# Scaling the residual rows during the up projection, with the second half's rows in buffers of their own

## The chip, the core and the metric

The kernel runs on one core of a Trainium2 chip. The core has five engines with instruction queues of their own: PE (matrix products; "PEld" in the profile is its loading of weights), DVE (elementwise work on vectors), ACT (activation functions and copies), POOL (elementwise work too) and SP, which computes nothing and issues DMA transfers. ACT and POOL can issue transfers as well. Each queue runs in order: an instruction that waits holds up everything behind it on the same engine. Engines wait for one another through semaphores.

The metric is device time in microseconds (us) of one execution.

## The reference

A trunk of two layers over 1024 tokens of 1024 features, in 32-bit floats. Layer 0 mixes with a gated delta rule, layer 1 with retention; each is followed by a feed-forward block with a short causal convolution. Every residual sum goes through a layer norm with a gain row `ln_g` and a bias row `ln_b`:

```
for i in range(2):
    sh1, sc1, g1, sh2, sc2, g2 = split(e @ ada_w[i] + ada_b[i], 6)
    y = mixers[i](x * (1 + sc1) + sh1)
    x = layer_norm(ALPHA * x + (1 + g1) * y, ln_g[i, 0], ln_b[i, 0])
    y = conv_ffn(x * (1 + sc2) + sh2, ffn_up[i], ffn_conv_w[i], ffn_conv_b[i], ffn_down[i])
    x = layer_norm(ALPHA * x + (1 + g2) * y, ln_g[i, 1], ln_b[i, 1])

def conv_ffn(h, w_up, conv_w, conv_b, w_down):
    gate, up = split(h @ w_up, 2)
    return (silu(causal_dwconv(gate, conv_w) + conv_b) * up) @ w_down
```

The point of the change is the `x` inside `ALPHA * x` of the second layer norm of each layer. What the kernel stores after the first norm is the normalized rows without gain and bias (`x_mid`, tensors `xs`), because the product that follows can take the gain into its own scale. The residual sum after the down projection needs the rows with gain and bias: x = n * g + b, row by row. Somebody has to compute that, for 1024 rows in each layer.

## The kernel before

**Products.** Each 32-bit product is made of three passes: a value is split into a coarse part (ACT, line 89) and the rest (DVE, line 90), and PE multiplies low by high, high by low and high by high. The large products use a seven-product scheme (Strassen and Winograd) on blocks of 512.

**Up projection** (`strassen`, called by `layer_tail`). It goes through 22 items, eleven pairs of a gate item and an up item. The first two are handled apart; the items from 2 on run in `wino`. An item loads two weight blocks into `wr` (lines 1223 and 1224, two buffers), forms seven products of 12 matmuls each, and hands four quarters to a `sink`. A gate item ends in the convolution (DVE line 1568), an up item in the gated quarters `o`, their four sums and differences on POOL (line 1589) and seven stores to DRAM (`ad`, line 1573, issued by SP). Twice in each item `bg_step` does one unit of background work from a list `bg`, for example a strip of the conditioning product `ada` (lines 215 to 243).

**Down projection** (`proj_gen`). Seven products over `nj` = 11 blocks, in the order 11, S1, S2, S4, 12, S3, 22. For each block SP loads a piece of the stored activations (`ar`, line 1274) and, three steps ahead, a piece of the weights (`Bw`, `Br`, line 1307); DVE forms differences (lines 1315 to 1321) and both are split. After each product its four accumulators are evacuated (`f1` to `f7`); the lines that matter are 1414 (`f3`), 1399 (`f2`) and 1421 (`f7`). The queue order of each engine is not written out by hand: a scheduler orders the instructions by program order and its own estimate of when each is ready, so that loads are often issued long before the place where they are written. `issue_after` (here `after(key)`) holds an instruction behind a named one on the same queue.

**The residual rows.** For the first half (512 rows) `xload(0, t)` loads four tiles of 128 rows from `x_mid` in the third product (S2), and DVE applies gain and bias in place, four operations for each tile (line 1357). For the second half `gain_half` (lines 1343 to 1350), eight times in the fourth and fifth products, loads 128 x 512 values into a buffer of the tag `xT` (two buffers), lets POOL multiply and add, and has POOL store them to the scratch tensor `xg`. `xload(1, t)` loads them back from `xg` in the sixth product, into the four buffers of the tag `lane`, which hold the first half's rows until these are stored. The gain rows are four tiles of the tag `auh` (eight buffers). That tag also serves the rows of the gate `rows[i, 5]`, the rotary tables `trig` (line 1636) and others.

`finish(half, t, nh, c)` then forms ALPHA * x + g * y (line 1364) and the norm's statistics, and `norm` normalizes; in the last layer (`final`) it also applies the output's gain and bias and stores the result.

For layer 1's first sum another route exists already: `bg_gain` puts 16 units into the background list; each loads 128 x 512 values into a `lane` buffer, scales them on POOL and has SP store them to `xg`.

Of the kernel before, what the change touches and what calls it, by code (L numbers as in the profile page):

```python
# [33 lines left out]
def trunk_kernel(ctx: ExitStack, tc, A):  # L34
# [84 lines left out]
    def bg_step(tile=mm_tile):  # L119
        bg_ps[0] = tile  # L120
        for p in pend:
            p[0] -= 1
        while pend and (pend[0][0] <= 0 or not bg):
            pend.pop(0)[1]()
            if not bg:
                break
        if bg:
            nxt = bg.pop(0)()
            if nxt:
                pend.append(list(nxt))  # L130

# [249 lines left out]
    def bg_gain(n, src, dst):  # L381
        gb = []

        def unit(c, r):
            if r == 0:
                gb[:] = [tl("auh", [P, HALF], name="gb") for _ in range(2)]
                for t, nm in zip(gb, ("ln_g", "ln_b")):
                    sp.dma_start(t, A[nm][n:n + 1, hs(c)].to_broadcast([P, HALF]))
            x = tl("lane", [P, HALF], name="xg")
            rs = slice(r * P, r * P + P)  # L390
            sp.dma_start(x, src[rs, hs(c)])
            if r == 7:
                return gain(x, rs, c)
            return 1, lambda: gain(x, rs, c)

        def gain(x, rs, c):
            pool.tensor_tensor(x, x, gb[0], ALU.mult)
            pool.tensor_tensor(x, x, gb[1], ALU.add)
            sp.dma_start(dst[rs, hs(c)], x)

        for c in range(2):
            for r in range(8):
                bg.append(lambda c=c, r=r: unit(c, r))
# [757 lines left out]
    def strassen(hT0, xts, scale, shift, items, tags=("hTb", "hTb", "qkv", "qkv", "aux"), direct=False):  # L1161
# [58 lines left out]
        def wino(n, sink):  # L1220
            ua, ub = items[n][:2]
            wa, wb = tl("wr", [P, D]), tl("wr", [P, D])
            sp.dma_start(wa, ua)
            sp.dma_start(wb, ub)
# [24 lines left out]
            bg_step()  # L1249

# [27 lines left out]
    def proj_gen(nj, ablk, wsrc, slots, xsrc, G, final, ln_next, tag, ltags, dst, key, mm=pe.matmul, gate=None, gain=None):  # L1278
# [62 lines left out]
        grows = gain_rows(gain[0], key) if gain else None  # L1341

        def gain_half(n):
            hf, rs = n // 4, slice(HALF + n % 4 * P, HALF + (n % 4 + 1) * P)
            x = tl("xT", [P, HALF], name="xg")
            with after("w"):
                sp.dma_start(x, gain[1][rs, hs(hf)])
            for r, op in zip(grows, (ALU.mult, ALU.add)):
                pool.tensor_tensor(x, x, r[hf], op)
            pool.dma_start(xsrc[rs, hs(hf)], x)  # L1350

        def xload(half, t):
            xt = load_row(xsrc if half or not gain else gain[1], half, t)
            if half == 0 and gain:
                for r, op in zip(grows, (ALU.mult, ALU.add)):
                    for hf in range(2):
                        dve.tensor_tensor(xt[:, hs(hf)], xt[:, hs(hf)], r[hf], op)
            xts[half].append(xt)
            stats[half].append(tl("st", [P, 2, 6]))

        def finish(half, t, nh, c):
            dve.tensor_tensor(c, c, G[nh], ALU.mult)
            xv = xts[half][t][:, hs(nh)]
# [3 lines left out]
        def norm(half, t):  # L1367
# [7 lines left out]
            else:  # L1375
# [3 lines left out]
                lo, hi = xt[:, hs(0)], xt[:, hs(1)]  # L1379
# [71 lines left out]
        for p, (an, bn, fin, side, fresh) in enumerate(prods):  # L1451
# [8 lines left out]
            for j in range(nj):  # L1460
# [8 lines left out]
                if gain and p in (3, 4) and j % 2 == 0 and j < 8:  # L1469
                    gain_half((p - 3) * 4 + j // 2)  # L1470
                if gain and p == 2 and j % 2 == 0 and j < 8:
                    xload(0, j // 2)
                if p == 2 and j < 4 and gate:
# [30 lines left out]
            if p == 4:  # L1504
                hooks = [] if final else ln_hooks(0, xts[0], tag, ln_next, outs, dst, key, bal["h"])
                hooks += [lambda t=t: xload(1, t) for t in range(4)]
# [12 lines left out]
    def layer_tail(i, mix, wout, xsrc, x_mid, x_out, ln_next, final):  # L1519
# [14 lines left out]
        bg_ada(i, 5, "row")  # L1534
        if i == 0:
# [7 lines left out]
        def pair_items(fp):  # L1543
# [31 lines left out]
            def up_start():  # L1575
                seen = []

                def gated(q, a, b):
# [7 lines left out]
                    if len(seen) == 4:  # L1586
# [8 lines left out]
        strassen(hT0, xts, sc2, sh2, [it for fp in range(NF // 2) for it in pair_items(fp)])  # L1595
        slots = {"c": "hTa", "x": "qkv"}
        gb2 = gain_rows(3, ("mid", i), "hTb") if final else None
        return proj_st(proj_gen(NF // 2, ablk_of(ad, "qkv"), A["ffn_down"][i], slots, xg[i + 1], rows[i, 5],
                       (gb2, x_out) if final else None, ln_next, "hTb", ("hTb", "hTa", 8, 6, "f") if final else ("qkv", "hTa", 8, 4, "0"), x_out, ("out", i), gain=(2 * i, x_mid)))
# [358 lines left out]
```

## Time and profile before

| what | value |
|---|---|
| median of 3 runs | 2968.27 us (2963.58 to 2969.49) |
| the profiled execution | 2955.5 us, of which the span of its instructions is 2953.7 us |
| granted TensorE clock, mean | 0.984 |
| PE busy / idle in the span | 2816.4 us / 137.3 us |
| DVE, ACT, POOL busy | 2243.3, 1318.0, 451.1 us |
| up projection, layer 0 and 1 | about 795 to 1193 us and 2325 to 2735 us |
| down projection, layer 0 and 1 | about 1193 to 1430 us and 2735 to 2935 us |

How to read the rows that follow. A row of the stage windows gives a stretch of the span, its length, then the busy time and number of instructions of PE, PEld, DVE, ACT and POOL, the granted clock, the share of the DMA engines' time in use, and GB/s. A row of the timeline gives start, duration, engine, line, operation and tiles (`out<-in`); a bracket at its end is the idle time before it and what ended that. A row of the waits reads "engine line <- what it waited for: total, times, longest". In the chain of waits each row is a start, a duration and the piece of work on the path that ended last. "SPq" is SP's queue. Tiles of one tag share a number of buffers; a new tile waits until an older one is released.

### The profile page before, as it was taken

Reading aid. Unit: us, or ns where it says so; the run is one execution under the profiler, and the core shown is the slowest. Engines: PE = TensorE matmul, PEld = TensorE weight load, DVE = VectorE, ACT = ScalarE, POOL = GpSimd, SP = SyncE. Lnnn points to the kernel's source line nnn. Section 1 sums busy time; section 2 is a strip of 40 time slices with the busy share of each in tenths; the row PEclk is TensorE's granted clock in tenths of the full one; section 3 lists DMA queues with packets and bytes.
Section 4 is the critical chain, followed back from the end, with each engine's and each line's share of the span. In section 5 each row is a group of like instructions: output and inputs, shape, how many; then the busy total and the mean of one; then the engine's idle time right before and its main releaser. Section 6 shows DMA issues by size and latency. Waiting matters only on the chain.

```text
span 2953.7 us, 38896 instructions
## 1 busy us (share of the span) xinstructions
PE 2816.4 (95%) x13638; PEld 2303.2 (78%) x13638; DVE 2243.3 (76%) x4005; ACT 1318.0 (45%) x2413; POOL 451.1 (15%) x469
## 2 busy tenths in 40 slices
PE   8998898999999999999999999999999899999997
PEld 7887777887788888877878877777777788888885
DVE  5788787656688888968676756666689787777989
ACT  4745565444544444545333333222244544445443
POOL 0302221100001111140000022422202011111211
PEclk9999999999999999999999999999999999999999
DMA  7231222254244445765343364755654343324763
GB/s 277 86 111 65 83 79 80 83 168 158 92 160 163 150 162 174 286 225 175 131 147 121 109 229 144 222 169 177 198 204 146 103 136 107 107 102 159 278 205 136
DMA packets 244403, 451.01 MB, mean 153 GB/s; under 512 B 23088, under 2 KB 76592, under 8 KB 244208
## 3 DMA queue, kind: packets, MB, share of 16 engines
q1 hardware_dynamic: 213088, 401.07, 41.1%
q10 hardware_dynamic: 29760, 43.00, 4.0%
q0 software_dynamic: 1360, 4.46, 0.4%
q8 instruction: 107, 1.75, 0.2%
q14 instruction: 88, 0.72, 0.1%
HBM read 339.91 MB, written 108.53 MB: 152 GB/s over the span
## 4 chain that ended last, share of the span: by engine, by line
PE 77%; DVE 9%; DMA 6%; ACT 4%; issue 2%; POOL 1%; SPq 0%; POOLq 0%; ACTq 0%; DVEq 0%
PE acc L655 15%; PE acc L1167 10%; PE acc L110 6%; PE acc L111 6%; PE acc L112 6%; PE sc L1167 5%; PE acc L1441 4%; PE sc L655 4%; PE mm L655 2%; PE sc L111 2%; PE sc L112 2%; PE sc L110 2%; PE mm L658 1%; DMA Br<-in_ffn_down 1%; PE acc L314 1%
## 5 line engine op out<-in xcount | busy, mean ns | idle before, releaser
L655 PE MATMUL acc<-hT,wh 128*128 128x512 f32 x960 | 300.1, 394 | 0.0
L1441 PE MATMUL acc<-bb,ab 128*128 128x512 f32 x984 | 233.4, 395 | 9.7 <-DVE bb L90 7.0
L1589 POOL TENSOR_TENSOR o<-o 128x512 f32<-128x512 f32 x80 | 112.3, 1414 | 793.6 <-DVE o L1582 494.0
L1441 PEld LDWEIGHTS acc<-bb,ab 128*128 128x128 f32 x984 | 183.7, 189 | 54.0 <-DVE bb L90 11.8
L1167 PE MATMUL acc<-T,wb 128*128 128x512 f32 x840 | 202.9, 390 | 6.5 <-DVE wb L90 6.5
L655 PEld LDWEIGHTS acc<-hT,wh 128*128 128x128 f32 x960 | 182.2, 190 | 34.1
L89 ACT ACTIVATE ab<-ar 128x512 fp32r<-128x512 f32 x210 | 130.4, 627 | 174.1 <-PE mm L291 57.4
L655 PE MATMUL acc<-hT,wl 128*128 128x512 f32 x480 | 201.2, 419 | 0.0
L1167 PEld LDWEIGHTS acc<-T,wb 128*128 128x128 f32 x840 | 157.0, 188 | 42.9 <-DVE wb L90 9.8
L90 DVE TENSOR_TENSOR wl<-wr,wh 128x1024 fp32r<-128x1024 f32 x95 | 123.3, 1298 | 81.9 <-ACT wh L89 81.6
L90 DVE TENSOR_TENSOR ab<-ar,ab 128x512 fp32r<-128x512 f32 x210 | 159.7, 765 | 30.0 <-ACT ab L89 29.9
L90 DVE TENSOR_TENSOR wb<-mm,wb 128x512 fp32r<-128x512 f32 x216 | 146.0, 684 | 26.4 <-ACT wb L89 25.5
L89 ACT ACTIVATE wh<-wr 128x1024 fp32r<-128x1024 f32 x95 | 100.8, 1062 | 142.8 <-PE acc L655 66.4
L90 DVE TENSOR_TENSOR wb<-wr,wb 128x512 fp32r<-128x512 f32 x162 | 110.5, 687 | 69.0 <-ACT wb L89 68.8
L1228 ACT ACTIVATE pc<-acc 128x512 f32<-128x512 f32 x143 | 84.9, 594 | 163.1 <-PE acc L1167 108.8
L1568 DVE SCALAR_TENSOR_TENSOR o<-g,vc,o 128x512 f32<-128x512 f32 (+2 forms) x176 | 145.6, 844 | 6.2 <-ACT o L1563 5.5
L89 ACT ACTIVATE wb<-mm 128x512 fp32r<-128x512 f32 x216 | 123.9, 595 | 53.8 <-DVE mm L1217 49.3
L89 ACT ACTIVATE wb<-wr 128x512 fp32r<-128x512 f32 x162 | 99.8, 629 | 99.7 <-DMA wr<-in_ffn_up 36.4
L655 PE MATMUL acc<-wh,hT 128*128 128x512 f32 x384 | 137.4, 420 | 2.9 <-DVE vv L90 1.7
L110 PE MATMUL acc<-T,wb 128*128 128x512 f32 x292 | 115.6, 396 | 9.4 <-DVE wb L90 9.4
L476 DVE SCALAR_TENSOR_TENSOR qkv<-raw,vc,qkv 128x512 f32<-128x512 f32 x144 | 111.7, 780 | 11.4 <-ACT qkv L474 10.7
L111 PE MATMUL acc<-T,wb 128*128 128x512 f32 x292 | 115.1, 394 | 0.0
(641 smaller groups left out, 7428.6 us busy)
## 6 DMA issues: line engine op xcount, KB each, us to landing
wr<-in_ffn_up SPq DMA_DIRECT2D x92, 512.0 KB, 4.2
mvw<-in_ada_w SPq DMA_DIRECT2D x80, 512.0 KB, 4.1
ad<-o SPq DMA_DIRECT2D x154, 256.0 KB, 3.1
ar<-ad SPq DMA_DIRECT2D x154, 256.0 KB, 4.8
Br<-in_ffn_down SPq DMA_DIRECT2D x88, 256.0 KB, 4.3
wr<-in_ret_wv SPq DMA_DIRECT2D x32, 512.0 KB, 4.1
ar<-od SPq DMA_DIRECT2D x56, 256.0 KB, 5.4
xs<-xt ACTq DMA_DIRECT2D x24, 512.0 KB, 3.6
```

What stands on the lines that cost most here:

```text
L89: act.activation(dst_h, src, AF.Copy)
L90: eng.tensor_tensor(dst_l, src, dst_h, ALU.subtract)
L110: mm(acc, wl[:, k], hl[0], start=first, stop=False)
L111: mm(acc, wh[:, k], hl[1], start=False, stop=False)
L112: mm(acc, wh[:, k], hl[0], start=False, stop=last)
L476: dve.scalar_tensor_tensor(oh, raw[:, 3 - j:515 - j], w[:, 3 - j:4 - j], oh, ALU.mult, ALU.add)
L655: pq(pe.matmul(out, lhsT, rhs, start=start, stop=stop), cost)
L1167: return pe.matmul(*a, skip_group_check=True, **kw)
L1228: act.activation(t, X, AF.Copy)
L1441: return pe.matmul(*args, skip_group_check=True, **kw)
L1568: dve.scalar_tensor_tensor(tv, gv[:, c0 - j:c1 - j], w[:, 2 - j:3 - j], tv, ALU.mult, ALU.add)
L1589: (dve if fp == 0 else pool).tensor_tensor(o[d], o[x], o[y], op)
```

## The change

Five things are done:

1. `bg_gain` gets a tag. With the tag `xT` its units go to a list of their own, `rowq`; their loads (and those of the gain rows) are held behind the current item's second weight load (`anchor["wi"]`), and POOL issues their stores.
2. `layer_tail` calls it with `x_mid` and `xg[i + 1]`, so that all 1024 rows of each layer are scaled; `row_step` takes one unit at the end of each item from number 5 on, and anything left after the last item.
3. `proj_gen` loses its `gain` parameter, the gain rows, `gain_half` and the scaling on DVE. Both halves are loaded from `xg`.
4. The first two tiles of the second half go into `xT` buffers.
5. In the last layer the second half is loaded in the fourth product (S4) in place of the sixth, and its other two tiles go into pairs of `auh` buffers.

```
+    rowq, rowp = [], []
+
+    def row_step():
+        if rowp:
+            rowp.pop()()
+        if rowq:
+            nxt = rowq.pop(0)()
+            if nxt:
+                rowp.append(nxt[1])
...
-    def bg_gain(n, src, dst):
+    def bg_gain(n, src, dst, tag="lane"):
...
-                for t, nm in zip(gb, ("ln_g", "ln_b")):
-                    sp.dma_start(t, A[nm][n:n + 1, hs(c)].to_broadcast([P, HALF]))
-            x = tl("lane", [P, HALF], name="xg")
+                with after("wi") if tag == "xT" else nullcontext():
+                    for t, nm in zip(gb, ("ln_g", "ln_b")):
+                        sp.dma_start(t, A[nm][n:n + 1, hs(c)].to_broadcast([P, HALF]))
+            x = tl(tag, [P, HALF], name="xg")
             rs = slice(r * P, r * P + P)
-            sp.dma_start(x, src[rs, hs(c)])
+            with after("wi") if tag == "xT" else nullcontext():
+                sp.dma_start(x, src[rs, hs(c)])
...
-            sp.dma_start(dst[rs, hs(c)], x)
+            (sp if tag == "lane" else pool).dma_start(dst[rs, hs(c)], x)
...
-                bg.append(lambda c=c, r=r: unit(c, r))
+                (bg if tag == "lane" else rowq).append(lambda c=c, r=r: unit(c, r))
...
-            sp.dma_start(wb, ub)
+            anchor["wi"] = sp.dma_start(wb, ub)
...
             bg_step()
+            if n > 4:
+                row_step()
...
-        grows = gain_rows(gain[0], key) if gain else None
-
-        def gain_half(n):
-            hf, rs = n // 4, slice(HALF + n % 4 * P, HALF + (n % 4 + 1) * P)
-            x = tl("xT", [P, HALF], name="xg")
-            with after("w"):
-                sp.dma_start(x, gain[1][rs, hs(hf)])
-            for r, op in zip(grows, (ALU.mult, ALU.add)):
-                pool.tensor_tensor(x, x, r[hf], op)
-            pool.dma_start(xsrc[rs, hs(hf)], x)
...
-            xt = load_row(xsrc if half or not gain else gain[1], half, t)
-            if half == 0 and gain:
-                for r, op in zip(grows, (ALU.mult, ALU.add)):
-                    for hf in range(2):
-                        dve.tensor_tensor(xt[:, hs(hf)], xt[:, hs(hf)], r[hf], op)
-            xts[half].append(xt)
+            if half and t < 2:
+                x = load_row(xsrc, half, t, tag="xT")
+            elif half and final:
+                x = two("auh", F32, "xt")
+                r0 = HALF + t * P
+                for hf in range(2):
+                    with after("w"):
+                        sp.dma_start(x[hf], xsrc[r0:r0 + P, hs(hf)])
+            else:
+                x = load_row(xsrc, half, t)
+            xts[half].append(x)
...
-                if gain and p in (3, 4) and j % 2 == 0 and j < 8:
-                    gain_half((p - 3) * 4 + j // 2)
-                if gain and p == 2 and j % 2 == 0 and j < 8:
+                if not gate and p == 2 and j % 2 == 0 and j < 8:
                     xload(0, j // 2)
+                if final and p == 3 and j % 2 == 0 and j < 8:
+                    xload(1, j // 2)
...
-                hooks += [lambda t=t: xload(1, t) for t in range(4)]
+                if not final:
+                    hooks += [lambda t=t: xload(1, t) for t in range(4)]
...
         bg_ada(i, 5, "row")
+        bg_gain(2 * i, x_mid, xg[i + 1], "xT")
...
         strassen(hT0, xts, sc2, sh2, [it for fp in range(NF // 2) for it in pair_items(fp)])
+        while rowq or rowp:
+            row_step()
...
-                       (gb2, x_out) if final else None, ln_next, ..., x_out, ("out", i), gain=(2 * i, x_mid)))
+                       (gb2, x_out) if final else None, ln_next, ..., x_out, ("out", i)))
```

A small helper `xh(half, t, nh)` picks the half of a row tile, whether it is one tile or a pair.

More of the change, by code (lines that the diff above doesn't have):

```diff
@@ L1276, in ablk_of, with proj_gen @@
         return ablk
-    def proj_gen(nj, ablk, wsrc, slots, xsrc, G, final, ln_next, tag, ltags, dst, key, mm=pe.matmul, gate=None, gain=None):
+    def proj_gen(nj, ablk, wsrc, slots, xsrc, G, final, ln_next, tag, ltags, dst, key, mm=pe.matmul, gate=None):
         bal = {nm: BAL[ltags[4] + nm] for nm in ABLK + ("w11", "w21", "w22", "wT1", "wT2", "wT3", "wT4", "n", "h")}
@@ L1340, in proj_gen, with xh @@
         stats = [[], []]
-        grows = gain_rows(gain[0], key) if gain else None
-        def gain_half(n):
-            hf, rs = n // 4, slice(HALF + n % 4 * P, HALF + (n % 4 + 1) * P)
-            x = tl("xT", [P, HALF], name="xg")
-            with after("w"):
-                sp.dma_start(x, gain[1][rs, hs(hf)])
-            for r, op in zip(grows, (ALU.mult, ALU.add)):
-                pool.tensor_tensor(x, x, r[hf], op)
-            pool.dma_start(xsrc[rs, hs(hf)], x)
-        def xload(half, t):
-            xt = load_row(xsrc if half or not gain else gain[1], half, t)
-            if half == 0 and gain:
-                for r, op in zip(grows, (ALU.mult, ALU.add)):
-                    for hf in range(2):
-                        dve.tensor_tensor(xt[:, hs(hf)], xt[:, hs(hf)], r[hf], op)
-            xts[half].append(xt)
+        def xload(half, t):
+            if half and t < 2:
[9 more added lines that the diff above has]
+            xts[half].append(x)
             stats[half].append(tl("st", [P, 2, 6]))
+        def xh(half, t, nh):
+            x = xts[half][t]
+            return x[nh] if isinstance(x, tuple) else x[:, hs(nh)]
         def finish(half, t, nh, c):
             dve.tensor_tensor(c, c, G[nh], ALU.mult)
-            xv = xts[half][t][:, hs(nh)]
+            xv = xh(half, t, nh)
             dve.scalar_tensor_tensor(xv, xv, ALPHA, c, ALU.mult, ALU.add)
@@ L1378, in norm @@
                 dve.scalar_tensor_tensor(mv[:, 2:3], mv[:, 0:1], -1.0, mv[:, 3:4], ALU.mult, ALU.mult)
-                lo, hi = xt[:, hs(0)], xt[:, hs(1)]
+                lo, hi = xh(half, t, 0), xh(half, t, 1)
                 act.activation(hi, hi, AF.Identity, bias=mv[:, 2:3], scale=mv[:, 3:4])
@@ L1598, in layer_tail @@
         return proj_st(proj_gen(NF // 2, ablk_of(ad, "qkv"), A["ffn_down"][i], slots, xg[i + 1], rows[i, 5],
-                       (gb2, x_out) if final else None, ln_next, "hTb", ("hTb", "hTa", 8, 6, "f") if final else ("qkv", "hTa", 8, 4, "0"), x_out, ("out", i), gain=(2 * i, x_mid)))
+                       (gb2, x_out) if final else None, ln_next, "hTb", ("hTb", "hTa", 8, 6, "f") if final else ("qkv", "hTa", 8, 4, "0"), x_out, ("out", i)))
     g1 = two("auh", F32, "g1")
```

## The prediction

> **What bounds the kernel now.** I read the page first, then the chain of waits, the PE queue and the stage windows of the two feed-forward layers.
>
> ```profile
> span 2953.7 us, 38896 instructions
> PE 2816.4 (95%) x13638; PEld 2303.2 (78%) x13638; DVE 2243.3 (76%) x4005; ACT 1318.0 (45%) x2413; POOL 451.1 (15%) x469
> ```
>
> PE is the bound on average, and the change touches no matmul. It can only win back time in which PE waits, or make new waits. So the question is where PE waits inside the stages that change: the up projections from item 5 on and the down projections, in both layers. I went there with the stage windows (us; busy time and count of PE, PEld, DVE, ACT, POOL; clock, DMA share, GB/s).
>
> ```profile
> 942.00:981.00 39.00, 39.00 (x176) 32.30 (x175) 34.22 (x56) 18.73 (x39) 5.59 (x4) 1.00 0.48 157
> 2600.00:2640.00 40.00, 40.00 (x178) 33.10 (x178) 28.70 (x43) 18.55 (x32) 5.58 (x4) 1.00 0.34 119
> 1260.00:1330.00 70.00, 63.02 (x272) 51.78 (x271) 45.65 (x56) 26.30 (x46) 28.07 (x24) 0.95 0.67 226
> 1330.00:1400.00 70.00, 65.58 (x298) 52.28 (x296) 62.37 (x114) 42.53 (x72) 4.82 (x4) 1.00 0.52 169
> 2870.00:2900.00 30.00, 30.00 (x134) 24.86 (x133) 30.00 (x56) 16.13 (x29) 2.12 (x2) 1.00 0.54 167
> 2935.00:2953.70 18.70, 0.23 (x2) 0.00 (x0) 14.64 (x32) 2.44 (x3) 4.03 (x3) 0.62 0.25 98
> ```
>
> The up projections (first two rows) leave PE no idle time. The down projection of layer 0 leaves 7.0 us of 70 and then 4.4 of 70. That of layer 1 keeps PE busy to the end, but with DVE full (30.00 of 30), and it has a tail of 18.7 us with no PE work in which DVE is busy for 14.64. So layer 0's hole is the first thing to explain. The chain of waits there, in order of time (start, us, what):
>
> ```profile
> 1283.60 5.80 DMA xg<-xs
> 1289.55 1.68 POOL xg L1349
> 1291.29 1.30 POOL xg L1349
> ...
> 1292.88 3.98 DMA xg<-xg
> 1296.91 3.44 DMA xg<-xs
> ...
> 1303.76 5.29 DMA xg<-xg
> 1309.06 0.38 SPq L215
> 1309.54 5.14 DMA Br<-in_ffn_down
> ```
>
> This is `gain_half`: load half a row block, scale it on POOL, store it, and only then load the next one into the same `xT` buffer (there are two). The last link is a weight load that stood behind this on SP. What DVE and PE did with the late weight, and what SP waited for between 1240 and 1330 (total, times, longest):
>
> ```profile
> 1314.80 0.69 DVE L1321 TENSOR_TENSOR Br<-Bw,Br 128x512 f32<-128x512 f32 x1 [10.19 <-DMA Br<-in_ffn_down]
> 1321.41 0.68 DVE L1414 TENSOR_TENSOR u<-sc,u 128x512 f32<-128x512 f32 x1
> PE sc L289 <- DVE u L1414: 7.0, 1, 7.0
> SPq L1347 <- DMA xg<-xg: 19.8, 4, 7.4
> SPq L1636 <- POOL xg L1349: 8.2, 3, 3.8
> SPq L1307 <- DVE ab L90: 11.2, 4, 5.9
> ```
>
> DVE stood 10.19 us before a subtraction of a weight block; the evacuation of the finished product (L1414) was queued behind it, and PE needed those banks: 7.0 us lost. SP lost 19.8 us to the buffers of `gain_half` and 8.2 us to rotary tables that wait for the gain rows' buffers. Only 11.2 us is the ordinary wait for a weight buffer.
>
> **The change part by part.** Rows of the pieces that are moved or removed (ns min/median/max):
>
> ```profile
> L1357 DVE TENSOR_TENSOR xt<-xt,rowb x32: 677/681/686, 1234.6 to 2781.2; 128x512 f32<-128x512 f32 x32
> L1349 POOL TENSOR_TENSOR xg<-xg,rowb x32: 1280/1604/8602, 1253.1 to 2833.2; 128x512 f32<-128x512 f32 x32
> L1350 POOL DMA_DIRECT2D xg<-xg x16: 559/582/759, 1263.7 to 2834.8; - x16
> L1347 SPq DMA_DIRECT2D xg<-xs x16: 319/372/435, 1250.1 to 2828.1; - x16
> ```
>
> 1. Removed from DVE: 32 in-place scalings, 16 x 0.68 = 10.9 us per layer. They fall at 1235 to 1257 and before 2782, where PE does not wait; credited at 0. The work that hides them is the product PE has in hand.
>
> 2. Removed from the down projection: 8 loads on SP, 16 POOL operations and 8 stores per layer. In layer 0 the 10.19 us wait of DVE loses its cause, and with it the 7.0 us of PE: **-7.0**. Bounds: 0, if SP is then late through something else (its 11.2 us for weight buffers, the `L215` load that also stands in the chain), and -11.4, if the 4.4 us of the next window go too. I take the first hole whole and the second not at all: in 1330 to 1400 DVE has 62.37 of 70 to do, and its work there is unchanged, so what is late next after the stall goes is DVE in the sixth product.
>
> 3. Layer 1, same part. SP's wait, DVE's two waits for late rows, and the chain of the tail:
>
> ```profile
> SPq L1347 <- DMA xg<-xg: 4.1, 2, 3.6
> 2840.18 0.69 DVE L1321 TENSOR_TENSOR Br<-Bw,Br 128x512 f32<-128x512 f32 x1 [1.46 <-DMA Br<-in_ffn_down]
> 2921.41 4.08 DMA out_dram<-xt
> 2925.51 3.89 DMA xt<-xg
> 2924.87 0.69 DVE L1364 SCALAR_TENSOR_TENSOR xt<-xt,pa 128x512 f32<-128x512 f32 x1 [1.10 <-issue]
> 2929.49 0.69 DVE L1364 SCALAR_TENSOR_TENSOR xt<-xt,pa 128x512 f32<-128x512 f32 x1 [0.98 <-DMA xt<-xg]
> ```
>
> From 2840 DVE sets the end, so time that it stands idle after that is time of the kernel. The second half's rows are loaded into `lane` buffers that become free only when the first half's output is stored (4.08, then 3.89 for the load). In the new kernel they are loaded during the fourth product, before the row at 2840, two into `xT`, two into `auh`: DVE's 1.10 + 0.98 go, **-2.1**. The 1.46 at 2840 follows SP's block of 3.6 by `gain_half`: **-1.5**. Bounds for both: 0, and -5.4 if early rows also let the four rows' last two DVE steps of the upper half (8 x 0.68) move ahead of PE's end; DVE is full before it, so I do not count on that. The four early loads add 2 MB on SP and the DMA engines in the place where 2 MB of loads and 2 MB of stores leave: 0. In layer 0 the first two rows of the second half go to `xT` and no longer wait for `lane`; nothing waited there: 0.
>
> 4. Added to the up projections: per layer 16 units, one per item from 5 on, each a 256 KB load on SP, two POOL operations of 1.3 us or more, one store issued by POOL (0.58); twice per layer two gain rows. An item is 7 x 12 = 84 matmuls, so the first window above (x176) holds a pair of items, 19.5 us each. A unit's round trip in the chain above was 5.80 + 1.68 + 1.30 + 3.98 = 12.8 us, with two buffers: SP should not stand for `xT`. The load is queued behind the second weight load of its item, so that weight is not delayed; DMA is busy to 0.48. POOL has 5.59 us to do in 39 us and gets 2 x 3.2 more. Queued behind a unit on POOL are the four sums of L1589, behind them on SP their stores and then the next weights: a unit that waits for its load could delay these, but the second weight load of the item below left SP at 956.45 and its four sums came at 967.12, 10.7 us later. 0 for all of that; if the cover is gone, an item loses what the unit is late.
>
> What is left is DVE, which slows while POOL works. Rows of one pair of items, and a block with a short lead:
>
> ```profile
> 956.45 0.62 SPq L1224 DMA_DIRECT2D wr<-in_ffn_up  x1
> 967.12 5.80 POOL L1589 TENSOR_TENSOR o<-o 128x512 f32<-128x512 f32 x4 [32.71 <-DVE o L1582]
> 971.68 1.78 DVE L1568 SCALAR_TENSOR_TENSOR o<-g,vc,o 128x511 f32<-128x511 f32 x1
> 973.99 0.73 DVE L1568 SCALAR_TENSOR_TENSOR o<-g,vc,o 128x510 f32<-128x510 f32 x1
> 950.76 0.69 DVE L90 TENSOR_TENSOR wb<-mm,wb 128x512 fp32r<-128x512 f32 x1
> 952.79 2.88 PE L1167 MATMUL sc<-T,wb 128*128 128x512 f32 x12
> ```
>
> Beside POOL one DVE operation took 1.78 instead of 0.73: 1.05 us. A unit has two POOL operations, so between 0 and 2.1 us. The block that PE starts at 952.79 was ready at 951.45, a lead of 1.34 us, in a gate item in which DVE runs without a gap. So a unit costs PE between 0 and 2.1 - 1.34 = 0.76 us. I take 0.3 for the 8 gate items of layer 0, where DVE has 34.22 of 39 to do, and 0 elsewhere (28.70 of 40 in layer 1): **+2.4**. Bounds 0 and 32 x 0.76 = 24.3.
>
> Sum: -7.0 - 2.1 - 1.5 + 2.4 = -8.2 us. The profiled execution took 2955.5 us (span 2953.7 and 1.8 around it), so 2947.3 by its measure; the median of the runs is 2968.27, 12.8 above it, and the same difference gives **2960.1 us**.
>
> **The rivals.**
>
> A, POOL blocks DVE in every unit (slower). All 32 units cost PE the full 0.76: +24.3 against -10.6, that is +13.7, 2982. It decides from 0.33 + 5.9/32 = 0.52 us per unit. For it: DVE's busy share in layer 0 and the long stretch without a gap. Against it: the four sums of L1589 already do this once per pair, and PE lost nothing in those windows; and the delay must meet a short lead. The Trainium skill, "SBUF — State Buffer", section "Who interferes with whom", says that a DVE instruction with two SBUF inputs and a GpSimd instruction that reads SBUF hold a shared port in turn, the second blocked until the first ends. By that rule a unit could hold DVE for two whole POOL operations, 2 x 1.28 - 1.34 = 1.2 us for PE, and 32 x 1.2 - 10.6 = +28. The 1.78 row agrees in kind; that every unit meets a two-input operation twice, no row shows. I give A 0.19.
>
> B, the change doesn't remove the stall. SP stays late in layer 0 through weight buffers, the `L215` load and the rotary tables, and PE loses the same 7.0 at the same place. Left: -3.6 + 2.4 = -1.2, 2967. For it: layer 1 has a 1.46 wait for the same kind of weight with only 4.1 us of SP lost to `xg`. Against it: SP waited 28 us for `gain_half` and its rows, 11.2 for weight buffers. 0.23.
>
> C, the order of the queues improves throughout: with SP early, the hole of 4.4 in 1330 to 1400 goes too, and the tail by 5.4 instead of 2.1: -7.0 - 4.4 - 5.4 - 1.5 + 2.4 = -15.9, 2952. For it: the chain in that window has loads as well as DVE. Against it: DVE's 62.37 of 70. 0.10.
>
> **How the numbers follow.** My forecast 0.48, B 0.23, A 0.19, C 0.10. Its own range is 2955 to 2965. The whole range runs from 2949 (C and a little) to 2976, which takes in B and the lower half of A. A measurement here tells about 0.2%, 5.9 us, from no change: the forecast is beyond it in most of its range, C wholly, B not, A mostly. Faster 0.53, same 0.28, slower 0.19.
>
> **What would show it.** Right: no POOL scaling after 1200 in layer 0, no DVE wait near 10 us at the fourth product's end, PE idle under 2 us between 1260 and 1330; in layer 1 DVE without waits for `xt` after 2840 and a tail under 17 us. In the up projections, PE's matmul count per 40 us unchanged within 2. Wrong: PE gaps of half a us in items 5 to 20, a weight block that DVE finishes just as PE starts it, or SP standing at the new row loads. A PE wait for L1414 that stays, with SP waiting for weight buffers, would be B.

## The result and the profile after

| | kernel before | changed kernel |
|---|---|---|
| median | 2963.58 us (2952.21 to 2969.49, 7 runs) | 2951.72 us (2944.43 to 2956.7, 7 runs) |
| ratio of the times | | 0.9962, 95% interval 0.9944 to 0.998 |
| the profiled execution, its span | 2955.5, 2953.7 us | 2954.0, 2952.2 us |

The change saves 11.9 us (0.4%), yet the two profiled executions differ by only 1.5 us. The profile before came from near the low end of its kernel's times, and most of what follows hangs on that.

The page after, the stage windows (columns as before) and, for 1240 to 1330, what SP's queue waited for:

```profile
span 2952.2 us, 38981 instructions
...
PE 2822.2 (96%) x13638; PEld 2306.3 (78%) x13638; DVE 2212.5 (75%) x3973; ACT 1316.4 (45%) x2413; POOL 494.4 (17%) x517
```

```profile
942.00:981.00 39.00, 39.00 (x174) 31.97 (x173) 34.16 (x51) 18.65 (x38) 12.25 (x10) 1.00 0.54 178
1260.00:1330.00 70.00, 70.00 (x311) 57.96 (x310) 43.80 (x70) 32.07 (x57) 0.00 (x0) 1.00 0.52 158
1330.00:1400.00 70.00, 64.01 (x279) 51.28 (x277) 57.86 (x106) 40.00 (x67) 4.54 (x5) 0.95 0.54 173
2935.00:2952.20 17.20, 1.23 (x6) 0.69 (x4) 12.91 (x27) 2.44 (x3) 3.21 (x3) 0.63 0.31 122
```

```profile
SPq L1288 <- DVE ab L90: 27.6, 17, 3.8
SPq L1321 <- DVE ab L90: 19.6, 12, 5.0
```

The hole of layer 0 is gone (PE 70.00 of 70, 311 matmuls where there were 272), and SP waits there for ordinary weight and activation buffers alone. But the next window became worse: 279 matmuls where there were 298. The item pair in the first row runs 174 matmuls where it ran 176, the most that the prediction allowed for. The tail, from the end of PE's last matmul (2936.2 us, before 2935.2) to the end of the span, takes 16.0 us where it took 18.5.

In layer 1 the subtraction that had waited 1.46 us waits 0.29, and `finish` on the row tiles (now L1377) runs with no idle time in front of it (DVE's timeline):

```profile
2840.78 0.69 DVE L1335 TENSOR_TENSOR Br<-Bw,Br 128x512 f32<-128x512 f32 x1 [0.29 <-DMA Br<-in_ffn_down]
...
2921.07 0.68 DVE L1377 SCALAR_TENSOR_TENSOR xt<-xt,pa 128x512 f32<-128x512 f32 x1
...
2923.48 1.89 DVE L1377 SCALAR_TENSOR_TENSOR xt<-xt,pa 128x512 f32<-128x512 f32 x3
```

PE executes nearly the same queue in all these kernels, so the start of the matmul with a given number marks the same stage in each. From these marks come the stage lengths below (us). "up 0" runs from 80 matmuls ahead of item 2 to the first matmul of layer 0's down projection, "up 1" from the first matmul of item 2 to that of layer 1's down projection. Then come three products of layer 0's down projection, and layer 1's last product with the tail. The medians take unprofiled and profiled executions together; the kernel before had 2964.83, 2964.33, 2962.06 and 2964.52 in the four later batches.

```
kernel                     median   span    up 0   4th    5th    6th    up 1   last+tail
before                    2963.58  2953.7  414.3  37.06  31.41  36.87  392.4  51.6
e9  before again                -  2965.3  415.5  45.61  32.68  37.66  392.0  50.2
after                     2951.72  2952.2  418.0  29.92  29.92  42.34  392.3  48.0
e1  after again           2953.11  2950.8  418.1  29.92  29.92  41.44  395.1  47.3
e2  layer 0 only          2955.65  2956.3  420.3  29.92  29.92  38.17  391.4  51.7
e3  layer 1 only          2959.86  2957.3  414.9  46.99  31.52  38.63  394.5  46.1
e4  before, POOL loads    2958.42  2954.7  422.4  29.92  29.92  35.66  395.9  50.4
e5  late rows             2954.12  2951.3  422.9  29.92  29.92  35.33  394.5  49.2
e6  no units              2946.46  2941.7  415.0  29.92  29.92  41.39  391.4  47.3
e7  units, no arithmetic  2946.45  2945.4  414.4  29.92  29.92  41.69  391.4  47.6
e8  layer 0's rows in 4th 2949.05  2952.0  418.6  29.92  29.92  37.08  395.3  46.2
e10 layer 0's rows late   2950.87  2948.7  425.7  29.92  29.92  35.12  394.5  46.5
e11 units on DVE          2958.06  2960.2  426.1  29.92  29.92  42.73  395.1  47.5
e12 e10, units earlier    2952.43  2955.0  426.3  29.92  29.92  34.98  395.8  46.4
```

29.92 is a product of 132 matmuls without a hole; the sixth has 24 small ones besides. The table is single executions; where three or more of one kind agree I use it as a finding, and a lone difference of a few us not.

### The profile page after: what moved, and what is told of

Its sections match the earlier page's. It is cut to its first block, busy times and chain, and to the rows that moved or that the text cites. A ratio compares the mean times of both kernels' runs of the same rounds, so it can differ in the third digit from the quotient of the medians.

```text
span 2952.2 us, 38981 instructions
## 1 busy us (share of the span) xinstructions
PE 2822.2 (96%) x13638; PEld 2306.3 (78%) x13638; DVE 2212.5 (75%) x3973; ACT 1316.4 (45%) x2413; POOL 494.4 (17%) x517
## 4 chain that ended last, share of the span: by engine, by line
PE 73%; DVE 13%; DMA 6%; ACT 4%; issue 2%; POOL 1%; SPq 0%; POOLq 0%; ACTq 0%; DVEq 0%
PE acc L667 15%; PE acc L1179 9%; PE acc L110 5%; PE acc L111 5%; PE acc L112 5%; PE sc L1179 4%; PE sc L667 4%; PE acc L1454 3%; PE mm L667 3%; PE sc L111 2%; PE sc L112 2%; PE sc L110 2%; DVE o L1583 1%; PE mm L1454 1%; PE sc L1454 1%
## 5 line engine op out<-in xcount | busy, mean ns | idle before, releaser
L1454 PEld LDWEIGHTS acc<-bb,ab 128*128 128x128 f32 x984 | 186.4, 191 | 56.1 <-DVE bb L90 15.5
L1179 PE MATMUL acc<-T,wb 128*128 128x512 f32 x840 | 203.2, 391 | 6.3 <-DVE wb L90 6.2
L90 DVE TENSOR_TENSOR ab<-ar,ab 128x512 fp32r<-128x512 f32 x210 | 148.5, 713 | 65.2 <-ACT ab L89 65.2
L409 POOL TENSOR_TENSOR xg<-xg,gb 128x512 f32<-128x512 f32 x48 | 62.6, 1304 | 776.3 <-DMA xg<-xs 453.1
L1583 DVE SCALAR_TENSOR_TENSOR o<-g,vc,o 128x512 f32<-128x512 f32 (+2 forms) x176 | 154.7, 896 | 5.3 <-ACT o L1578 4.7
L110 PE MATMUL acc<-T,wb 128*128 128x512 f32 x292 | 116.0, 397 | 9.4 <-DVE wb L90 9.4
L488 DVE SCALAR_TENSOR_TENSOR qkv<-raw,vc,qkv 128x512 f32<-128x512 f32 x144 | 111.7, 780 | 11.5 <-ACT qkv L486 10.7
```

Source lines behind the costliest of these rows:

```text
L90: eng.tensor_tensor(dst_l, src, dst_h, ALU.subtract)
L110: mm(acc, wl[:, k], hl[0], start=first, stop=False)
L488: dve.scalar_tensor_tensor(oh, raw[:, 3 - j:515 - j], w[:, 3 - j:4 - j], oh, ALU.mult, ALU.add)
L1179: return pe.matmul(*a, skip_group_check=True, **kw)
L1454: return pe.matmul(*args, skip_group_check=True, **kw)
L1583: dve.scalar_tensor_tensor(tv, gv[:, c0 - j:c1 - j], w[:, 2 - j:3 - j], tv, ALU.mult, ALU.add)
```

## The experiments

### One layer at a time

**e1_both_again**: the changed kernel, unedited.

> The changed kernel once more, for a second profile and a tighter ratio. The two profiles so far differ by 1.5 us, the medians by 11.9. Theory: what repeats is layer 0's fourth product without its 7 us hole (about -8.6 us from item to item of PE's work), a few tenths of a us per item lost in layer 0's up projection (3.7 us in all), and layer 1's end 4 to 5 us earlier; the 5.8 us given back in layer 0's sixth product is partly chance, so that stage will read somewhere between 7 and 13 us of PE gaps. Ratio 0.995 to 0.998. Rival: the hole in layer 0 moves into the sixth product whatever happens; then the sixth product gives back 5 to 6 us again and the ratio comes from layer 1 alone, 0.998 to 0.999.

**e2_layer0_only** and **e3_layer1_only**: both paths stand in the kernel and `NEW` says which layer takes the new one.

```
+NEW = (0,)          # e3: (1,)
...
+        if i in NEW:
+            bg_gain(2 * i, x_mid, xg[i + 1], "xT")
...
-             ..., x_out, ("out", i)))
+             ..., x_out, ("out", i), gain=None if i in NEW else (2 * i, x_mid)))
```

> The change in layer 0 alone; layer 1 keeps its scaling in the down projection. Theory: the fourth product's hole goes (-8.6) and the up projection costs 3.7; if the sixth product gives nothing back, -5 us, ratio 0.998; if it gives back 5.8, about +1 us, ratio 1.000. Rival: if the whole gain of 11.9 us sits in layer 0, ratio 0.996.

> The change in layer 1 alone; layer 0 keeps its scaling in the down projection, with its hole of 7 us. Theory: -4.6 us at the end, +1 in the up projection: -3.6 us, ratio 0.9988. Rival: the whole gain of 11.9 us sits in layer 1 and the hole in layer 0 only moves: ratio 0.996. Together with the run of layer 0 alone the two parts should add up to the change.

Measured: both 2953.11 (ratio 0.9966, 0.9954 to 0.9978), layer 0 alone 2955.65 (0.9973, 0.996 to 0.9986), layer 1 alone 2959.86 (0.998, 0.9965 to 0.9995), against 2964.83. Gains of 9.2 and 5.0 us, which add up to 14.2 where both together give 11.7, no more apart than the intervals allow: each layer pays on its own account, layer 0 by the medians about twice as much. e1's ratio is in the range of its theory, but the long sixth product repeated (41.44 after 42.34), so it was not the chance that the theory took it for in part. e2's interval leaves out the 1.000, and e3's the rival's 0.996; e2's reaches from its theory's 0.998 to the rival's 0.996.

e3 leaves layer 0 as before, so it holds a second execution of the old hole, and it is far larger than the first. Waits in 1240 to 1345:

```profile
DVE Br L1336 <- DMA Br<-in_ffn_down: 17.7, 3, 16.6
...
PE sc L300 <- DVE u L1444: 16.9, 1, 16.9
```

DVE waits 16.6 us for a weight block and PE 16.9 behind it, at the place where the first profile showed 10.19 and 7.0.

### The kernel before, once more

**e9_before_again** is the kernel before without an edit.

> The kernel before, unchanged, for a second profile of it. If the hole at the end of layer 0's fourth product differs between executions and explains why the kernel before scatters over 17 to 19 us in its times: the fourth product takes something between 30 and 47 us here (37.06 in the first profile, 46.99 where layer 0 was left as it was), and the rest of the span stands within 3 us of the first profile's, stage by stage. If the scatter comes from the whole kernel: the fourth product takes 37 again and other stages differ by more than 3 us.

Its execution took 2967.03 us. The chain of waits (start, us, what), PE's wait, and the window behind the hole in this execution:

```profile
1301.66 1.50 POOL xg L1349
...
1303.22 1.63 POOL xg L1349
...
1305.14 3.87 DMA xg<-xg
...
1309.07 3.58 DMA xg<-xs
...
1315.75 4.29 DMA xg<-xg
1320.05 0.38 SPq L215
...
1320.53 5.39 DMA Br<-in_ffn_down
```

```profile
PE sc L289 <- DVE u L1414: 15.5, 1, 15.5
```

```profile
1333.30:1341.00 7.70, 7.65 (x22) 6.10 (x23) 7.52 (x13) 0.00 (x0) 0.00 (x0) 0.63 0.27 96
```

It is the same chain as in the first profile, link for link: a row block scaled on POOL and stored, the buffer reloaded, scaled and stored again, then the weight load. It ends 11 us later, and PE waits 15.5. Stage by stage the rest of the span stands within 2.2 us of the first profile's, as the first reading expected. So the hole is what differs between these two executions. It does not make the whole scatter of the kernel's times: they reach from 2952 to 2972 us, but those of the changed kernel, which has no such hole in either of its profiles, still from 2944 to 2958.

The hole also costs after it has ended. In the 7.7 us behind it PE ran 22 matmuls at a granted clock of 0.63; in the first profile 28 at 0.81 (first row below), and without a hole 36 at 1.00 (second row, the changed kernel):

```profile
1322.20:1330.00 7.80, 7.76 (x28) 6.36 (x29) 7.61 (x13) 0.00 (x0) 0.00 (x0) 0.81 0.28 97
```

```profile
1319.60:1327.40 7.80, 7.80 (x36) 6.47 (x35) 7.80 (x14) 1.84 (x5) 0.00 (x0) 1.00 0.36 109
```

That is the fifth product's excess: 31.41 - 29.92 = 1.5 us in the first profile, 2.8 in the second. The whole price was 7.1 + 1.5 = 8.6 us there, 15.7 + 2.8 = 18.5 here, and 17.1 + 1.6 = 18.7 in e3. The Trainium skill, "TensorE: Matmul & The Clock Gate", Part 1, says that the array falls to half its clock after an idle window of about 3.4 us and comes back after one that is busy; the rows agree in kind (matmuls 0.43 us apart instead of 0.23 for 3 and for 6 us).

### Is it SP's queue? e4_pool_loads

The kernel before, with the loads of `gain_half` issued by POOL. The round trip, the two buffers and POOL's work stay; only SP no longer stands for them.

```
-            with after("w"):
-                sp.dma_start(x, gain[1][rs, hs(hf)])
+            pool.dma_start(x, gain[1][rs, hs(hf)])
```

> The kernel before, with one edit: the loads of the second half's row blocks are issued by POOL in place of SP, so that SP no longer stands for their buffers; everything else of the scaling stays in the down projection, POOL's work beside DVE's too. Theory (SP's queue was the cause): DVE's wait of 10.19 us for the weight goes, PE's hole at the end of layer 0's fourth product falls from 7 us to under 2, and the time is about 7 us below the kernel before, ratio 0.997 to 0.998. Rival (DVE was late because it shares its time with POOL's row scaling, operations of 1.2 us in place of 0.68): the hole stays above 5 us, ratio 1.000.

Measured: 2958.42 (0.9983, 0.997 to 0.9996), and SP's waits in 1240 to 1330 begin with

```profile
SPq L1307 <- DVE ab L90: 18.6, 13, 5.0
SPq L1274 <- DVE ab L90: 15.1, 17, 3.8
```

The fourth product takes 29.92: one line removes the hole, so the cause was SP standing for the `xT` buffers, and neither POOL's speed nor the rows themselves. The median falls only 6.4 us all the same. Its profile has, before any edited instruction, a wait of PE for a split weight block (800 to 822):

```profile
PE acc L110 <- DVE wb L90: 9.8, 1, 9.8
```

The kernel before, the changed one, e7 and e12 lose 4.85 us at that place, e4 9.99 (the gap between two matmuls' starts beyond the usual 0.227). The edit has changed DVE's order there, through the scheduler. At the same place of layer 1's up projection, at 2335 us, it loses 9.46 in place of 4.85. That takes back about 10 us of what the hole's removal won, in one execution.

### What the units cost: e6, e7, e11

**e6_no_units** drops the units; the residual then lacks gain and bias.

```
-        bg_gain(2 * i, x_mid, xg[i + 1], "xT")
...
-        return proj_st(proj_gen(NF // 2, ..., slots, xg[i + 1], rows[i, 5],
+        return proj_st(proj_gen(NF // 2, ..., slots, x_mid, rows[i, 5],
```

> The changed kernel without the scaling units: no loads, POOL operations or stores of rows in the up projections; the down projections read the unscaled normalized rows. It leaves out gain and bias of the first norm in the residual sum. It prices what the units cost where they are put. Theory: layer 0's up projection from item 5 on gets back 3 to 4 us (414.3 in place of 418 us between the two marks), layer 1's 0 to 1; about 4 us under the changed kernel, ratio to the kernel before 0.995. Rival (the units are hidden): both stages as in the changed kernel, ratio 0.9966.

**e7_no_arith** keeps the units' loads and stores and leaves out POOL's two operations (gain and bias).

```
-            pool.tensor_tensor(x, x, gb[0], ALU.mult)
-            pool.tensor_tensor(x, x, gb[1], ALU.add)
+            if tag == "lane":
+                pool.tensor_tensor(x, x, gb[0], ALU.mult)
+                pool.tensor_tensor(x, x, gb[1], ALU.add)
```

> The changed kernel with the units' loads and stores kept and their two POOL operations left out, so the rows are stored unscaled. It leaves out gain and bias of the first norm in the residual sum. It parts the two ways in which a unit can cost time. Theory (POOL's operations slow DVE's operations beside them, 1.78 in place of 0.73 us): layer 0's up projection gets back the same 3 to 4 us as without the units. Rival (the transfers delay the items' weights): it stays as slow as in the changed kernel, 418 us or more.

**e11_dve_units** gives the two operations to DVE.

```
+            eng = pool if tag == "lane" else dve
+            eng.tensor_tensor(x, x, gb[0], ALU.mult)
+            eng.tensor_tensor(x, x, gb[1], ALU.add)
```

> The changed kernel, with the units' two operations done by DVE in place of POOL, in both layers. Leaving POOL's operations out gave PE 17 matmuls more in 800 to 1190 us (3.9 us) and none in layer 1. Theory 1: what counts is DVE's total time. DVE gets 16 x 2 x 0.68 = 21.8 us a layer in place of the 6 to 9 us by which POOL slowed it, so layer 0 gets worse: under 1670 matmuls between 800 and 1190, and the median rises to 2955 or more. Theory 2: what counts is that POOL's operations meet short-lead operations of DVE at a time that no queue order decides, while DVE operations of its own are put where DVE has slack: 1690 or more matmuls in that window, median 2946 to 2950. In layer 1 both expect no change of PE in the up projection.

Medians: 2946.46 without units, 2946.45 without arithmetic, 2958.06 with the arithmetic on DVE (ratios 0.9944, 0.9948, 0.9988; intervals 0.9928 to 0.996, 0.993 to 0.9965, 0.9975 to 1.0002). So loads and stores cost nothing that can be seen, and by the medians the arithmetic costs 5 to 7 us. Their intervals overlap in part with the changed kernel's; the stages carry the reading. Layer 0's up projection takes 418.0 to 426.3 us in the seven profiles with the units' arithmetic on POOL (418.0 to 420.3 in the four without the holes of e5, e10 and e12 told below), and 414.3 to 415.5 in the five without arithmetic in it, e4 with its late weight block apart. The same 190 us of layer 0's up projection before, after, in e7 and in e11:

```profile
960.00:1150.00 190.00, 190.00 (x849) 157.34 (x849) 163.97 (x260) 92.69 (x189) 27.93 (x20) 1.00 0.48 156
```

```profile
960.00:1150.00 190.00, 189.86 (x843) 155.53 (x842) 166.50 (x254) 90.32 (x185) 61.30 (x50) 1.00 0.58 195
```

```profile
960.00:1150.00 190.00, 190.00 (x850) 157.34 (x849) 161.72 (x257) 92.00 (x187) 33.34 (x30) 1.00 0.59 196
```

```profile
960.00:1150.00 190.00, 185.35 (x821) 151.61 (x820) 166.90 (x266) 86.54 (x180) 32.88 (x29) 1.00 0.58 191
```

849, 843, 850, 821 matmuls: POOL's arithmetic costs 7, or 1.6 us in this stretch, without an idle time of PE that the eye would find (189.86 of 190); over the whole stage 418.0 - 414.4 = 3.6. DVE does six instructions fewer (254 for 260) in more time. One group shows it, the splits of fresh weights on DVE over 800 to 1190, after and in e7:

```profile
L90 DVE TENSOR_TENSOR wb<-wr,wb 128x512 fp32r<-128x512 f32 x57 | 42.9, 752 | 9.3 <-ACT wb L89 9.2
```

```profile
L90 DVE TENSOR_TENSOR wb<-wr,wb 128x512 fp32r<-128x512 f32 x58 | 39.8, 686 | 12.4 <-ACT wb L89 12.0 <-PE acc L1180 0.3
```

752 ns against 686. On DVE the arithmetic is dearer: 32 operations of 0.68 us there (21.8 us), and the stage loses 426.1 - 414.4 = 11.7 us. The first theory held for layer 0. In layer 1 the arithmetic costs about the same on either engine (395.1 us here, 392.3 to 395.8 on POOL). Part of layer 0's price is that DVE now waits for the units' loads: 6.0 us over the stage.

The Trainium skill, "SBUF — State Buffer", section "Who interferes with whom", has DVE's two-input operations and GpSimd take turns at a shared port. The slower splits fit that. Its full price, which stood in the prediction as +28, did not come: 3.6 us in 16 units of layer 0 is 0.23 us a unit.

### The early rows: e5, e8, e10, e12

**e5_late_rows**: the second half's rows of both layers back in `lane` buffers, loaded in the sixth product.

```
-            if half and t < 2:
-                x = load_row(xsrc, half, t, tag="xT")
-            elif half and final:
...
-            else:
-                x = load_row(xsrc, half, t)
+            x = load_row(xsrc, half, t)
...
-                if final and p == 3 and j % 2 == 0 and j < 8:
-                    xload(1, j // 2)
...
-                if not final:
-                    hooks += [lambda t=t: xload(1, t) for t in range(4)]
+                hooks += [lambda t=t: xload(1, t) for t in range(4)]
```

> The changed kernel with the second half's rows loaded as before: all four into the buffers of the first half, in the sixth product, in both layers. The scaling stays in the up projections. Theory (the early rows end layer 1 sooner): layer 1's last product and tail together go from the changed kernel's 47 to 48 us back towards the 51.6 us of the kernel before, 3 to 4 us, and DVE waits for these rows again near the end; the rest as in the changed kernel; ratio to the kernel before 0.998. Rival (the tail shortens because SP and DVE are free of the scaling, whatever the buffers): 47 to 48 us stay, ratio 0.9966. In layer 0, if the two early tiles cause the give-back in the sixth product, its stage falls from 41 to 42 us to 37.

**e8_early_l0**: layer 0's two `xT` tiles loaded already in the fourth product, as in layer 1.

```
-                if final and p == 3 and j % 2 == 0 and j < 8:
+                if not gate and p == 3 and j % 2 == 0 and j < (8 if final else 4):
                     xload(1, j // 2)
...
-                    hooks += [lambda t=t: xload(1, t) for t in range(4)]
+                    hooks += [lambda t=t: xload(1, t) for t in range(0 if gate else 2, 4)]
```

> The changed kernel with layer 0's two early tiles of the second half loaded in the fourth product, as layer 1 does, in place of just before the sixth product's weights. Theory of the give-back (1 MB of rows issued by SP at 1341 us stands in front of the sixth product's weights, and DVE then waits 1.5 to 2.2 us four times for weights): layer 0's sixth-product stage falls from 41 to 42 us to about 38, ratio to the kernel before 0.9955. Rival (DVE has 62 of 70 us to do there and is the bound): the stage stays at 41 to 42 us, ratio 0.9966.

**e10_late_l0**: layer 0 as in e5, layer 1 as in the changed kernel (`if half and t < 2 and final`).

> The changed kernel, with the second half's first two row tiles of layer 0 in `lane` buffers again (as before the change); layer 1 keeps its early rows. Theory: in layer 0 the early rows cost time, since their loads go out in front of weight loads in the sixth product; the five profiles with them take 38.2 to 42.3 us for that product, the four without 35.3 to 38.6. Then the sixth product takes 35 to 37 us here, DVE waits less than 3 us for Br in it, layer 1's last product and tail keep their 47 to 48 us, and the median is 2947 to 2950 (ratio about 0.995). Rival: the sixth product's length is chance or is given back behind it; then the median is 2951 to 2954 as the changed kernel's.

Medians 2954.12, 2949.05 and 2950.87 (ratios 0.9969, 0.9952 and 0.9958; intervals 0.9958 to 0.9979, 0.9934 to 0.997, 0.9942 to 0.9974). All overlap the changed kernel's. The stages are clearer. With the early tiles in the sixth product it takes 38.2 to 42.7 us (six profiles); with late ones, or loads in the fourth product, 35.0 to 38.6 (eight; e8's 37.08 is about what its theory expected). The seventh product does not make up for it: both together take 74.4 to 77.0 us in the six and 68.4 to 71.8 in the eight. In the changed kernel the two row loads go out in front of the product's weight loads; SP's queue there, then DVE's waits in 1350 to 1395, after and in e10, then the chain after:

```profile
1340.59 0.33 SPq L1321 DMA_DIRECT2D Br<-in_ffn_down  x1
1341.02 0.86 SPq L294 DMA_DIRECT2D xt<-xg  x2
1342.90 0.32 SPq L1288 DMA_DIRECT2D ar<-ad  x1
```

```profile
DVE Br L1335 <- DMA Br<-in_ffn_down: 5.6, 3, 2.2
```

```profile
DVE Br L1335 <- DMA Br<-in_ffn_down: 2.6, 5, 1.1
```

```profile
1370.57 6.24 DMA Br<-in_ffn_down
...
1377.52 0.69 DVE bb L90
1378.25 4.27 PE acc L1454 x12
```

DVE waits 5.6 us in place of 2.6 for weights, and PE starts late and then runs 12 matmuls in 4.27 us, where 12 at full rate take 2.72. Undoing the edit removes the loss, so the early rows cause it in layer 0; by which path (SP's queue, or the row loads' share of the DMA engines) the runs don't say.

Why, then, does e10's median gain nothing? Its up projection is 7.7 us longer than the changed kernel's. SP's queue and its wait in 1158 to 1174, and the chain, in e10:

```profile
1167.46 0.38 SPq L225 DMA_DIRECT2D mvw<-in_ada_w  x1
1167.93 1.42 SPq L1588 DMA_DIRECT2D ad<-o  x3
```

```profile
SPq L225 <- DMA xg<-xg: 3.3, 1, 3.3
```

```profile
1168.45 0.38 SPq L1588
1168.92 5.11 DMA ad<-o
1174.20 0.56 issue
...
1175.35 0.50 ACT pc L1240
1175.89 4.21 PE acc L1179 x9
```

After the change the same stores stand before that load:

```profile
1164.21 1.69 SPq L1588 DMA_DIRECT2D ad<-o  x3
1165.95 0.61 SPq L225 DMA_DIRECT2D mvw<-in_ada_w  x1
```

A load of conditioning weights waits 3.3 us, by the profile for a unit's store; the gated rows' stores behind it come late, ACT waits for their buffers, and PE stands 3.4 us (its gap), then runs slowly. e5 has the same gap, 3.05 at 1174. Nobody edited this place: the scheduler only drew another order.

**e12_late_l0_units_early** starts the units two items earlier to change that order (`if n > 2:` in place of `if n > 4:`).

> As e10_late_l0, with the units started two items earlier (from item 3 in place of 5), so that SP's order at the end of layer 0's up projection has no conditioning load in front of the seven stores of item 19 any more. In e10 and in e5_late_rows SP waited 3.3 us with such a load for a unit's store at 1165, the gated rows' stores and the next weight came late, and PE lost 3.38 and 3.05 us at 1175. Theory: that hole took back what the sixth product won. Then PE has no gap over 1 us between 1150 and 1195 here, the sixth product takes 35 to 37 us, and the median is 2945 to 2948.5 (ratio 0.994 to 0.995). Rival: what is won in one place goes in another again (a new hole of 3 us or more somewhere in the up projection); then the median is 2950 to 2953.

2952.43 (0.9961, 0.9947 to 0.9975): the rival held. The sixth product stays short (34.98), and the hole moved with the units to 1140, waits and SP's queue as in e10:

```profile
SPq L225 <- DMA xg<-xg: 3.3, 1, 3.3
```

```profile
1132.24 0.38 SPq L225 DMA_DIRECT2D mvw<-in_ada_w  x1
1132.71 2.44 SPq L1588 DMA_DIRECT2D ad<-o  x3
```

So I have no version that is shown to beat the changed kernel; e8's 2949.05 is the lowest of those that compute everything, and lies within the interval.

## Why the prediction came out as it did

2960.1 was forecast and 2951.72 measured: inside the range of 2949 to 2976 and faster as forecast, but below the forecast's own range of 2955 to 2965, with a gain of 11.9 us against 8.2. Of the 8.4 us between the two times 4.7 come from the kernel before, whose median is 2963.58 over seven runs and was 2968.27 over three. The time is the one that rival C gave (2952), but C's mechanism did not come: the window behind the hole lost time where C had it win 4.4. That the time lies inside the range is in part luck, since the errors have opposite signs: the hole was larger than its term, and the sixth product and the units took more than theirs. Term by term, the stage table against it:

- **Layer 0's hole, -7.0.** Cause right: e4 removes it by taking `gain_half`'s loads off SP. Rival B falls with the profile after, where PE is busy for 70.00 of the 70 us. The size was read from the mildest of three executions, and without the slow matmuls behind it: 8.6 us in the profile before, 18.5 in e9. The failed step stands at the end of the sum: "the median of the runs is 2968.27, 12.8 above it, and the same difference gives 2960.1". I carried the 12.8 over as if it lay outside the change. With the median of seven runs it is 8.1, and a good part of that is likely the hole itself, which the change takes away: e9's execution, at 2967.03, is 11.5 above the first and its hole costs 9.8 more.
- **The next window, 0.** "What is late next after the stall goes is DVE in the sixth product" named the place and missed cause and sign: DVE had less to do (57.86 for 62.37) and waited for weights. The product became 5 us longer.
- **Layer 0's early rows, 0.** "Nothing waited there" looked at the rows and not at what their loads are put in front of. This is where those 5 us come from.
- **Layer 1, -2.1 and -1.5.** By the profiles the last product and tail went from 51.6 and 50.2 to 48.0 and 47.3, some 3 us. The tail behind PE's last matmul takes 17.6 to 18.7 us in the five profiles without early rows in layer 1, e5 (18.1) among them, and 14.3 to 16.0 in the nine with them. In e5 DVE waits 1.1 and 0.6 us before `finish` again, as before the change. So the early rows shorten the tail, by about what was forecast; e5's median, with an up projection that is 5 us longer in layer 0, doesn't tell. The wait at 2840 was worth 0.9 (30.82 to 29.92 for the fourth product).
- **The units, +2.4.** 3.6 us in layer 0. In layer 1, costed at 0, the up projection takes 392.3 us in this execution and 394.5 to 395.8 in the six other profiles with units on POOL there, where e6 and e7 take 391.4: 0.9 more in the one, 3 to 4 in the six. With layer 0 that comes near the 5 to 7 of the medians. The mechanism (DVE slowed beside POOL, short leads) is what e7 shows for layer 0. One sign that the prediction named for being wrong came: PE has a gap of 1.1 us at 915, behind a weight block of DVE (e9, without units, has one of 0.6 there). Rival A had the mechanism and some four times the size, 24.3.

Against e9, a more typical execution of before, the changed profile's stages add up as follows: fourth and fifth product -18.5, layer 1's down projection and tail -3.2 (of which -1.0 ahead of its last product), sixth product +4.7, up projections +2.5 and +0.2, the products and the norm just ahead of layer 1's up projection +2.0, all else -0.8: -13.1, the difference of the spans. The +2.0 is not repeated by e1, the same program, which has +0.3 there. Of 22 us won, 7 are given back in layer 0, a third: to POOL's arithmetic beside DVE, and to row loads among weight loads. What the units cost in layer 1 in the six other profiles comes on top.

## What to carry to other kernels

A stall that depends on when transfers land has no one size: before it is put into a sum, ask whether the profiled execution is a typical one, and if its time lies at an end of the runs, take the difference as a part of the stall and not as a constant. In a queue that issues in order, the cost of a transfer that waits is what stands behind it: moving the waiting load to another queue cured this one with one line, and moving the rows early put two others in front of weights. Where a scheduler draws the queues, compare whole stages and not only the edited place; four of these kernels (e4, e5, e10, e12) lost 3 to 5 us at places that no one had touched, e4 in both layers.

## What was not expected of the hardware

A wait of PE costs more than its length: behind gaps of 7.1, 15.7 and 17.1 us (before, e9, e3) matmuls came 0.43 us apart in place of 0.23, which added 1.5, 2.8 and 1.6 us, so the addition did not grow with the gap. The granted clock over the 7.8 and 7.7 us behind the first two was 0.81 and 0.63. And one stall of one fixed program was 7.1 us long in one execution and 15.7 in another.
